# Two-layer trunk on one core: operands of six early pairs before the right sums, later turns, and two of four W sums on POOL

## The chip, the cores and the metric

The kernel runs on one core of one Trainium2 chip. The core has five engines with a queue of instructions each: PE (TensorE, the matmuls), DVE (VectorE), ACT (ScalarE), POOL (GpSimd) and SP (SyncE, which here only issues DMAs). An engine takes its queue strictly in order; an instruction that waits for a semaphore holds up all behind it. The metric is device microseconds of one execution, lower is better; the value compared is the median of the runs.

## The reference, cut to what matters

A decoder trunk: 1024 tokens of width 1024, two layers. Layer 0 mixes tokens with a sparse attention (NSA), layer 1 with sliding-window attention with sinks (SWA); each is followed by a squared-ReLU MLP of hidden width 4096. All is float32.

```python
def squared_relu_mlp(h, w_up, w_down):
    a = jax.nn.relu(h @ w_up)
    return (a * a) @ w_down

for i in range(DEPTH):                       # DEPTH = 2
    ...                                      # mod = adaLN of the condition, six parts
    h = modulate(rms_norm(x, norm_g[i, 0]), sh1, sc1)
    y = nsa_mixer(h, ...) if i % N_MIXERS == 0 else swa_sink_mixer(h, ...)
    x = x + (1 + g1)[:, None, :] * rms_norm(y, norm_g[i, 1])
    h = modulate(rms_norm(x, norm_g[i, 2]), sh2, sc2)
    y = squared_relu_mlp(h, mlp_w_up[i], mlp_w_down[i])
    x = x + (1 + g2)[:, None, :] * rms_norm(y, norm_g[i, 3])
```

## The kernel before, in words

**Precision.** A float32 product is three matmuls (`mm3`, L572 to L574): each operand is split into a rounded part `hi` (a copy on ACT) and the rest `lo` (a subtraction), and hi*hi, lo*hi and hi*lo are summed.

**Tokens and tiles.** The tokens are 8 tiles of 128. When the attention of a tile is done, its output is projected, normed and added to x, and a second norm gives `xr` (`norm_stages`, L450 to L472). Then the tile is turned: PE transposes `xr` by 8 matmuls with the identity (L1234), and ACT scales and shifts it out of PSUM into the raw operand `hr` (L1245). The function `done` decides when: in before the turn's steps follow the norm by `DL` = 4 steps of the program, and the further ones by 1 step each.

**MLP up.** `h @ w_up` is done with one level of Strassen-Winograd: both operands are cut in 2x2 blocks, and seven products p = 1 to 7 take the place of eight. The blocks on the right side (R) are of tokens and depth: b11 and b21 are of tiles 0 to 3 (depth halves 0 and 1), b12 and b22 of tiles 4 to 7. R of p=1 is b11, of p=2 b21; p = 6, 5, 7 need the sums (b22 - (b12 - b11)), t1 = (b12 - b11) and (b22 - b12), p=3 needs b22, and p=4 needs b21 minus that of p=6. Each sum comes in two halves j of 128x1024 (`minus`, L1257), each R operand as hh on ACT (L1250) and hl on DVE (L1251). The left side (W) comes in 16 pairs of hidden blocks. A pair needs four sums of W blocks (`prep`, L1313, L1314, L1320 for p=7, L1324 for p=3, 128x512 each), and for each product a `wt`: hi on ACT (L1330), lo by a subtraction (L1331; on POOL for the early products, on DVE for the others). One product is 12 matmuls of 128x512. L1358 adds a product's PSUM bank on DVE into the pair's two accumulators `u` (a and b), ACT does the squared ReLU (L1370, L1371), and POOL adds the results up as the right side of the next Strassen level (`combine`: sx at L1403, sy at L1414), which SP stores.

**Order.** Products p=1 and p=2 need only tiles 0 to 3, so those of `PAIRS0` = 5 pairs (10 products) run first, while the last tiles are still normed and turned. Then come 6, 5, 7, 3, 4 of each of these pairs, then all seven of each later pair. `before(i)` places the preparation of product i + `AHEAD` (3) ahead of product i; `lead` holds what stands ahead of the first. Program order is only the start: the framework schedules each engine's queue by a simulated timeline, and the queues that result are fixed.

**Buffers.** W of a pair is loaded as two tiles of 512 KB by SP (L547), c=0 (w11, w21) into one of 3 "raw" buffers and c=1 (w12, w22) into one of 41 general slots of 4 KB per partition (`SLOTS`). R operands, `wt`, `u`, `sx` and early raw sums all live in the same slots. A slot is used again when the last reader of its tile is done; for an `sx` that is the landing of its store. In before the second tile of the third pair's W (`w_11048` in layer 0) stands in the slot of the first pair's accumulator b.

## Time and profile before

| what | value |
|---|---|
| runs | 2559.64, 2564.80, 2564.22 us; median 2564.22 us |
| profiled execution | 2561.28 us, span 2559.3 us, mean granted clock 0.972 |
| busy share | PE 94%, DVE 76%, ACT 55%, POOL 50% |
| attention and projection of layer 0, up to the first product of its MLP | up to about 889 us |
| MLP up of layer 0 | 889 to 1216 us |
| SWA attention of layer 1, with its turns | 1620 to 1930 us |
| MLP up of layer 1 | from about 1910 us |

PE is busy for most of the span. What can be won lies in the stretches where PE idles or runs at a lower clock. The profile's list of waits says what ended each idle time of PE, the timeline gives each instruction with its start and duration, and the table of stretches gives the granted clock (1.00 is 2.4 GHz, 0.50 is 1.2 GHz) beside the busy times.

### The profile page before, as it was taken

What the parts mean: (1) busy time and instruction counts of PE and PEld (TensorE: products, weight loads), DVE (VectorE), ACT (ScalarE), POOL (GpSimd) and SP (SyncE); (2) the same over time, 40 slices, a digit from 0 to 9 for tenths busy, and PEclk for the clock granted to TensorE, in tenths of its full rate; (3) what the DMA queues carried; (4) which work ended last, traced back from release to release, by engine and by line L of the source; (5) the groups of instructions that cost most, each with busy time, mean ns of one, the idle gap of its engine ahead of it and who ended that gap; (6) DMA issues with size and microseconds to landing.
All of it is one profiled execution on the core that took longest, in us unless ns stands there. A gap on an engine that the chain in (4) does not pass through costs nothing.

```text
span 2559.3 us, 36576 instructions
## 1 busy us (share of the span) xinstructions
PE 2396.3 (94%) x11974; PEld 1996.3 (78%) x11974; DVE 1946.4 (76%) x3751; ACT 1397.0 (55%) x2959; POOL 1274.1 (50%) x1256
## 2 busy tenths in 40 slices
PE   6989899999998979999999999889787999999997
PEld 4789788888887867778778887767676788888886
DVE  7965479999895579888899777477647876787656
ACT  4632368898983544444444454378765454445433
POOL 4420566565662255334955613477545543494433
PEclk9999999999999989999999999989899999999999
DMA  7367623122227536555988564452223555587754
GB/s 277 116 220 243 215 79 96 39 90 66 72 67 165 148 127 215 197 185 181 359 312 309 203 215 148 124 157 68 65 67 120 201 170 179 179 308 251 228 185 171
DMA packets 237205, 436.08 MB, mean 170 GB/s; under 512 B 19204, under 2 KB 120792, under 8 KB 237016
## 3 DMA queue, kind: packets, MB, share of 16 engines
q1 hardware_dynamic: 208216, 404.39, 47.3%
q0 software_dynamic: 28800, 29.36, 4.7%
q8 instruction: 94, 1.54, 0.2%
q14 instruction: 95, 0.78, 0.1%
HBM read 319.38 MB, written 114.31 MB: 169 GB/s over the span
## 4 chain that ended last, share of the span: by engine, by line
PE 58%; DVE 16%; DMA 10%; issue 6%; POOL 4%; ACT 4%; SPq 1%; DVEq 0%; POOLq 0%; ACTq 0%
PE b L574 14%; PE b L573 14%; PE b L572 14%; PE b L880 5%; PE b L903 5%; PE o L925 4%; DMA adaw<-in_ada_w_dram 3%; DVE wt L1331 2%; DVE p L884 2%; DMA w<-in_mlp_w_up_dram 2%; DMA w<-in_nsa_w_in_dram 1%; DMA wr<-in_mlp_w_down_dram 1%; DVE u L1358 1%; DVE pT L910 1%; DVE ada L323 1%
## 5 line engine op out<-in xcount | busy, mean ns | idle before, releaser
L574 PE MATMUL b<-hh,wt 128*128 128x512 f32 x896 | 350.8, 395 | 25.1 <-POOL wt L1331 21.2
L572 PE MATMUL b<-hh,wt 128*128 128x512 f32 x896 | 354.4, 396 | 9.8 <-ACT wt L1330 9.8
L573 PE MATMUL b<-st,st 128*128 128x512 f32 x896 | 349.5, 390 | 5.4 <-DVE st L1477 5.4
L573 PE MATMUL b<-hl,wt 128*128 128x512 f32 x896 | 352.4, 393 | 0.0
L574 PE MATMUL b<-st,st 128*128 128x512 f32 x896 | 348.3, 389 | 0.0
L572 PE MATMUL b<-st,st 128*128 128x512 f32 x896 | 332.5, 390 | 1.6 <-DVE u L1358 1.6
L888 ACT ACTIVATE p<-p,nm 128x256 f32<-128x256 f32 (+7 forms) x384 | 251.2, 660 | 59.0 <-DVE nm L884 57.8
L1028 POOL TENSOR_SCALAR p<-p,rl,nsam 128x640 f32<-128x640 f32 (+7 forms) x256 | 200.4, 796 | 137.8 <-DVE rl L1026 96.8
L1477 DVE TENSOR_TENSOR st<-sr,st 128x1024 fp32r<-128x1024 f32 (+1 forms) x128 | 193.3, 1510 | 77.5 <-ACT st L1476 76.1
L1403 POOL TENSOR_TENSOR sx<-u,u 128x512 f32<-128x512 f32 x64 | 106.2, 1660 | 273.0 <-ACT u L1371 224.8
L910 DVE TENSOR_TENSOR pT<-b,pT 128x512 fp32r<-128x512 f32 (+1 forms) x334 | 215.4, 657 | 27.6 <-ACT pT L909 27.4
L574 PEld LDWEIGHTS b<-hh,wt 128*128 128x128 f32 x896 | 170.3, 190 | 66.1 <-POOL wt L1331 22.9
L1370 ACT ACTIVATE u<-u 128x512 f32<-128x512 f32 x128 | 80.6, 630 | 244.6 <-DVE u L1358 244.5
L909 ACT ACTIVATE pT<-b 128x512 fp32r<-128x512 f32 (+1 forms) x334 | 187.2, 580 | 43.1 <-PE b L903 36.9
L572 PEld LDWEIGHTS b<-hh,wt 128*128 128x128 f32 x896 | 170.3, 190 | 50.4 <-ACT wt L1330 15.9
L1476 ACT ACTIVATE st<-sr 128x1024 fp32r<-128x1024 f32 (+1 forms) x128 | 122.2, 955 | 158.8 <-PE b L573 104.8
L573 PEld LDWEIGHTS b<-st,st 128*128 128x128 f32 x896 | 168.2, 188 | 42.6 <-DVE st L1477 8.2
L903 PE MATMUL b<-ident,p 128*128 128x128 f32 x1296 | 195.9, 277 | 5.0 <-DVE nm L884 4.1
L1477 DVE TENSOR_TENSOR st<-wr,st 128x1024 fp32r<-128x1024 f32 (+1 forms) x128 | 181.8, 1420 | 20.8 <-ACT st L1476 18.1
L573 PEld LDWEIGHTS b<-hl,wt 128*128 128x128 f32 x896 | 170.0, 190 | 35.0
L572 PEld LDWEIGHTS b<-st,st 128*128 128x128 f32 x896 | 168.2, 188 | 37.3 <-DVE u L1358 2.3
L574 PEld LDWEIGHTS b<-st,st 128*128 128x128 f32 x896 | 168.2, 188 | 34.7
(276 smaller groups left out, 6183.6 us busy)
## 6 DMA issues: line engine op xcount, KB each, us to landing
adaw<-in_ada_w_dram SPq DMA_DIRECT2D x96, 512.0 KB, 4.7
sr<-s SPq DMA_DIRECT2D x96, 512.0 KB, 4.8
wr<-in_mlp_w_down_dram SPq DMA_DIRECT2D x96, 512.0 KB, 6.0
w<-in_mlp_w_up_dram SPq DMA_DIRECT2D x74, 512.0 KB, 4.2
s<-sx SPq DMA_DIRECT2D x64, 512.0 KB, 5.1
x<-x SPq DMA_DIRECT2D x48, 512.0 KB, 4.1
s<-u SPq DMA_DIRECT2D x64, 256.0 KB, 2.1
we<-in_mlp_w_down_dram SPq DMA_DIRECT2D x64, 256.0 KB, 4.0
```

Source lines behind the costliest of these rows:

```text
L572: mm(out, s[0], m[0], start=first, stop=False)
L573: mm(out, s[0], m[1], start=False, stop=False)
L574: mm(out, s[1], m[0], start=False, stop=last)
L880: self.nc.tensor.matmul(out, q[:, g], k[z], start=z == 0, stop=z == 1)
L888: self.nc.scalar.activation(p, p, AF.Exp, scale=-1.0, bias=nm, accum_out=l)
L903: nc.tensor.transpose(pt[:, g * P:(g + 1) * P], p[:, cols], self.ident)
L909: nc.scalar.activation(x[:, 0, 0:w], pt[:, 0:w], AF.Copy)
L910: nc.vector.tensor_tensor(x[:, 1, 0:w], pt[:, 0:w], x[:, 0, 0:w].bitcast(F32), op=ALU.subtract)
L1028: nc.gpsimd.tensor_scalar(ps[g], ps[g], rl[:, g:g + 1], gate[:, g, b:b + 1], op0=ALU.mult, op1=ALU.mult)
L1403: nc.gpsimd.tensor_tensor(z[n][:, k], x, y, op=op)
L1476: nc.scalar.activation(hi, r, AF.Copy)
L1477: nc.vector.tensor_tensor(lo, r, hi.bitcast(F32), op=ALU.subtract)
```

## The change

It has six parts. (1) `SLOTS` goes from 41 to 40, and three small tensors of the NSA attention move from a slot into constants. (2) `PAIRS0` goes from 5 to 6, so 12 products run first; the raw W of pairs 3 to 5 stands in slots, the W operands of the early products are prepared earlier (`when`), and their lo part is made on DVE. (3) The sums t1 and b22 - b12 are made tile by tile as tiles 4 to 7 are turned (`near`, pieces of 128x256, one on DVE and one on POOL for each j); after the last tile only b11 (DVE, twice 128x1024) and b21 (POOL, twice) are left. (4) The turn of a tile follows its norm by `TURN` = 10 steps in layer 0 and 20 in layer 1 (6 for the last tile). (5) Of the four W sums of each of the 16 pairs, those for p=7 and p=3 are made on POOL. (6) The side work (adaLN of later stages) is spread over the products from the 23rd on and not from the 11th.

```diff
--- before.py
+++ after.py
@@ -26,10 +26,11 @@
 HID = 4096
 EPS = 1e-6
 NEG = -1e30
-SLOTS = 41
+SLOTS = 40
 UT = HID // P
 LEAD_DOWN = 14
-PAIRS0 = 5
+PAIRS0 = 6
+TURN = (10, 20)
 SIDE2 = 40
 AHEAD = 3
 DL = 4
@@ -209,10 +210,9 @@
 
     def setup_late(self):
         nc, a = self.nc, self.a
-        both = self.slot("nsac")
-        self.pe = both[0:32, 0:256].rearrange("p (m z d) -> p m z d", m=2, z=2)
-        self.w2 = both[:, 256:768].rearrange("p (m c z d) -> p m c z d", m=2, c=2, z=2)
-        self.Kc = both[:, 768:1024].rearrange("p (h n) -> p h n", h=4)
+        self.pe = self.const([32, 2, 2, 64], "pe")
+        self.w2 = self.const([P, 2, 2, 2, 64], "w2")
+        self.Kc = self.const([P, 4, 64], "Kc")
         for z in range(2):
             nc.sync.dma_start(self.pe[:, :, z, :], a["nsa_cmp_pe"][0].rearrange("m l d -> l m d"))
             for m in range(2):
@@ -1256,19 +1256,28 @@
                 raw[out] = self.slot("hr", F32, [P, 2, 512])
             eng.tensor_tensor(raw[out], raw[x], raw[y], op=ALU.subtract)
 
+        b11, b21, b12, b22, t1 = (lambda j, n=n: (*n, j) for n in ((0, 0), (0, 1), (1, 0), (1, 1), (2, 0)))
+
+        def near(t, j):
+
+            if t1(j) not in raw:
+                raw[t1(j)] = self.slot("hr", F32, [P, 2, 512])
+            v = lambda n: raw[n][:, :, (t - 4) * P:(t - 3) * P]
+            nc.vector.tensor_tensor(v(t1(j)), v(b12(j)), v(b11(j)), op=ALU.subtract)
+            nc.gpsimd.tensor_tensor(v(b12(j)), v(b22(j)), v(b12(j)), op=ALU.subtract)
+
         def tile(t, xr):
             steps = [lambda c=c: (turn(t, xr, c), put(t, c)) for c in range(2)]
-            if t == 3:
-                steps += [lambda c=c, j=j: split((1, 2)[c], raw[0, c, j]) for c in range(2) for j in range(2)]
+            if t > 3:
+                steps.append(lambda: (near(t, 0), near(t, 1)))
             if t == 7:
                 V, G = nc.vector, nc.gpsimd
-                b11, b21, b12, b22, t1 = (lambda j, n=n: (*n, j) for n in ((0, 0), (0, 1), (1, 0), (1, 1), (2, 0)))
-                steps.append(lambda: [minus(e, *f(j)) for f in (lambda j: (t1(j), b12(j), b11(j)), lambda j: (b11(j), b22(j), t1(j)))
-                                      for j, e in ((0, V), (1, G))])
-                steps += [lambda j=j: (split(6, raw[b11(j)]), minus(G, b12(j), b22(j), b12(j))) for j in range(2)]
-                steps += [lambda j=j: (split(5, raw.pop(t1(j))), minus(G, b21(j), b21(j), b11(j)), raw.pop(b11(j))) for j in range(2)]
-                for p, b in ((7, b12), (3, b22), (4, b21)):
-                    steps += [lambda p=p, b=b, j=j: split(p, raw.pop(b(j))) for j in range(2)]
+                steps.append(lambda: [minus(V, b11(j), b22(j), t1(j)) for j in range(2)])
+                for p, b in ((6, b11), (5, t1), (7, b12), (3, b22)):
+                    if p == 5:
+                        steps.append(lambda: [minus(G, b21(j), b21(j), b11(j)) for j in range(2)])
+                    steps += [lambda p=p, b=b, j=j: split(p, raw[b(j)]) for j in range(2)]
+                steps += [lambda j=j: split(4, raw[b21(j)]) for j in range(2)]
             return steps
 
 
@@ -1283,7 +1292,7 @@
 
         def load(q, early):
             if early:
-                r = self.raw_weight(self.raw, w_up, list(range(KT)), 2 * q * P, P)
+                r = self.raw_weight(self.raw if q < 3 else self.slot, w_up, list(range(KT)), 2 * q * P, P)
                 r = r.rearrange("p (k c) -> p k c", k=KT)
                 wraw[q] = {11: r[:, 0:4], 12: r[:, 4:8]}
             else:
@@ -1306,7 +1315,7 @@
                 return sums[n]
 
             if p == 1:
-                r = w[11] if early else w[11]
+                r = w[11]
             elif p == 2:
                 r = w[12]
             elif p == 6:
@@ -1317,35 +1326,38 @@
                 r = sums.pop(1)
             elif p == 7:
                 r = new(3)
-                t(r, w.pop(11), w.pop(21), op=ALU.subtract)
+                nc.gpsimd.tensor_tensor(r, w.pop(11), w.pop(21), op=ALU.subtract)
                 sums.pop(3)
             elif p == 3:
                 r = new(4)
-                t(r, w.pop(12), sums.pop(2), op=ALU.subtract)
+                nc.gpsimd.tensor_tensor(r, w.pop(12), sums.pop(2), op=ALU.subtract)
                 sums.pop(4)
             else:
                 r = w.pop(22)
             s = self.slot("wt", F32R, [P, 2, 512])
             hi, lo = (four(s[:, y]) for y in range(2))
             nc.scalar.activation(hi, r, AF.Copy)
-            (nc.gpsimd if early else nc.vector).tensor_tensor(lo, r, hi.bitcast(F32), op=ALU.subtract)
+            nc.vector.tensor_tensor(lo, r, hi.bitcast(F32), op=ALU.subtract)
             left[i] = s
             if early and p == 2 or p == 4:
                 wraw.pop(q)
 
+
+        first = at[0]
+        when = lambda i: -1 if i < 3 else (i - 3) // 2 if i < first else max(i - first + 5, i - AHEAD) if i < first + 5 else i - AHEAD
+
         def before(i):
 
-            out = []
-            n = i + AHEAD
-            if 0 <= n < len(order):
-                out.append(lambda: prep(n))
-            out += [lambda q=q: load(q, True) for q in range(2, PAIRS0) if n == 4 * (q // 2) + q % 2 - 3]
+            out = [lambda n=n: prep(n) for n in range(len(order)) if when(n) == i]
+            if i in (0, 1, 2):
+                out += [lambda q=q: load(q, True) for q in (3 + i,) if q < PAIRS0]
             for q in range(n_q):
-                if n == at[q] - 2:
+                if i == (2 if q == 0 else when(at[q] - 2)):
                     out.append(lambda q=q: load(q, False))
             return out
 
-        lead = [lambda q=q: load(q, True) for q in range(2)] + [f for i in range(-AHEAD, 0) for f in before(i)]
+        lead = [lambda q=q: load(q, True) for q in range(3)] + [lambda j=j: split(1, raw[b11(j)]) for j in range(2)] + \
+            before(-1) + [lambda j=j: split(2, raw[b21(j)]) for j in range(2)]
         return tile, (R, order, before, left, lead)
 
     def mlp_up(self, up, side, sd, begin):
@@ -1423,7 +1435,7 @@
             own = spread(before(i), product(i))
             if p == 4:
                 own.append(lambda q=q: self.later(lambda: self.chain(combine(q)), 1))
-            (ramp if i < 2 * PAIRS0 else steps).extend(own)
+            (ramp if i < 2 * PAIRS0 + 10 else steps).extend(own)
         self.go(ramp)
         self.go(spread(side, steps[:-LEAD_DOWN]) + spread(begin, steps[-LEAD_DOWN:]))
 
@@ -1709,10 +1721,9 @@
 
             take, up = self.up_setup(a["mlp_w_up"][l], lambda l=l: self.cols[l, 1])
 
-            def done(t, x, take=take, xr=xr):
+            def done(t, x, take=take, xr=xr, l=l):
                 def turn():
-                    for k, f in enumerate(take(t, xr)):
-                        self.later(f, DL if k == 0 else 1)
+                    self.chain([lambda: None] * (2 + DL if t == NT - 1 else TURN[l]) + take(t, xr))
                 self.chain(self.norm_stages(x, xr, t) + [turn])
 
             if l == 0:
@@ -1731,7 +1742,6 @@
                     return {26: loads[0:1], 27: loads[1:2], 28: loads[2:3], 29: loads[3:5], 30: loads[5:6], 31: loads[6:]}.get(n, [])
 
                 self.nsa_attention(more, parts[-1][1][QN:])
-                self.pe = self.w2 = self.Kc = self.Vc = self.cmask = self.fmask = self.gate = None
                 outs = [self.out_steps(t, lambda t=t: load(t), src[t], gate, x1[t], done) for t in range(NT)]
                 self.mark("wout")
                 outs[0][0]()
```

On POOL at the entry of layer 0's MLP, before (`hr` are raw operands and their sums, `wt` the lo part of an early product, `sx` and `sy` the first pair's results):

```order
L1331 TENSOR_TENSOR wt2399_10684<-w2382_10582,wt2399_10684 128x512
L1257 TENSOR_TENSOR hr2405_10725<-hr2351_10424,hr2240_9919 128x1024
L1257 TENSOR_TENSOR hr2350_10421<-hr2353_10432,hr2350_10421 128x1024
L1257 TENSOR_TENSOR hr2240_9919<-hr2354_10435,hr2405_10725 128x1024
L1257 TENSOR_TENSOR hr2351_10424<-hr2354_10435,hr2351_10424 128x1024
L1257 TENSOR_TENSOR hr2242_9927<-hr2242_9927,hr2239_9916 128x1024
L1331 TENSOR_TENSOR wt2408_10734<-w2378_10547,wt2408_10734 128x512
L1257 TENSOR_TENSOR hr2243_9930<-hr2243_9930,hr2240_9919 128x1024
L1331 TENSOR_TENSOR wt2422_10780<-w2382_10582,wt2422_10780 128x512
```

The same place on POOL after (`ws` are the sums of W blocks of the first two pairs):

```order
L1267 TENSOR_TENSOR hr2344_10413<-hr2347_10430,hr2344_10413 128x2x128
L1267 TENSOR_TENSOR hr2345_10416<-hr2348_10433,hr2345_10416 128x2x128
L1257 TENSOR_TENSOR hr2259_10002<-hr2259_10002,hr2256_9985 128x1024
L1257 TENSOR_TENSOR hr2260_10005<-hr2260_10005,hr2257_9988 128x1024
L1329 TENSOR_TENSOR ws2450_10945<-w2413_10764 128x512
L1333 TENSOR_TENSOR ws2453_10966<-w2414_10766,ws2444_10906 128x512
L1329 TENSOR_TENSOR ws2467_11050<-w2457_10979 128x512
L1333 TENSOR_TENSOR ws2471_11074<-w2458_10981,ws2462_11009 128x512
L1426 TENSOR_TENSOR sy2478_11098<-u2391_10659,u2455_10971 128x512
L1415 TENSOR_TENSOR sx2470_11071<-u2391_10659,u2455_10971 128x512
```

No lo part of a `wt` stands behind the full-size sums any more, two of which are left; four W sums stand ahead of the first pair's results.

On PE in the SWA attention, at the turn of the third tile, before (`xr` is the normed tile, `b` a PSUM bank, L880, L903 and L925 are attention matmuls):

```order
L574 MATMUL b3980_18653<-wh3703_17478,ol3958_18577 128x512
L925 MATMUL o3978_18649<-pT3955_18569,V23534_16476 128x512
L1234 MATMUL b3981_18666<-ident_67,xr3975_18633 128x128 x4
L1234 MATMUL b3982_18675<-ident_67,xr3975_18633 128x128 x4
L880 MATMUL b3983_18684<-K23530_16472,qs3962_18586 128x256 x4
L880 MATMUL b3984_18685<-K23530_16472,qs3962_18586 128x256 x4
```

The same place on PE after, with the rows where that tile's turn now stands:

```order
L574 MATMUL b3980_18669<-wh3703_17494,ol3958_18593 128x512
L880 MATMUL b3997_18758<-K23530_16488,qs3962_18602 128x256 x4
L925 MATMUL o3993_18742<-pT3977_18662,V23534_16492 128x512
...
L574 MATMUL b4003_18782<-wh3752_17674,ol3958_18593 128x512
L1234 MATMUL b4022_18881<-ident_67,xr3975_18649 128x128 x4
L1234 MATMUL b4024_18899<-ident_67,xr3975_18649 128x128 x4
```

The turn of `xr3975` went 36 rows down the list (a row being one matmul or a group of like ones), behind the next tile's projection products.

On SP in layer 0's MLP up, the issue of the second W tile of the third pair and what stands around it, before:

```order
L1415 DMA s2387_0_10621<-sy2476_11051 128x512
L547 DMA w2516_11289<-in_mlp_w_up_dram 128x4x256
L1409 DMA s2387_0_10621<-sx2468_11024 128x1024
L547 DMA w2475_11048<-in_mlp_w_up_dram 128x4x256
L1412 DMA s2387_0_10621<-sx2473_11043 128x1024
```

After:

```order
L1427 DMA s2387_0_10636<-sy2478_11098 128x512
L1421 DMA s2387_0_10636<-sx2470_11071 128x1024
L547 DMA w2477_11095<-in_mlp_w_up_dram 128x4x256
L1424 DMA s2387_0_10636<-sx2475_11090 128x1024
```

The place is nearly the same, but the buffer is another. `w2477_11095` stands in the slot that `sx2470_11071` leaves, so its load waits for the landing of the store one row above it, where before it waited for POOL's last read of an accumulator. Layer 1 has the same (`w_20251` in the slot of `sx_20227`; before, `w_20186` took the slot of an old `wt`). The second tile of the fourth and of the fifth pair stands in the slot of the accumulator b of two pairs earlier, in both layers.

## Rows read from the trace of the kernel before

**Rows 1.** The page: its first line, the span and the count of instructions.
```profile
span 2559.3 us, 36576 instructions
```
**Rows 2.** Timeline of POOL, 893 to 928 us: start, duration, engine, line, names, idle before.
```profile
899.97 14.99 POOL L1257 TENSOR_TENSOR hr<-hr,hr 128x1024 f32<-128x1024 f32 x5 [2.19 <-ACT hr L1245]
914.93 2.25 POOL L1331 TENSOR_TENSOR wt<-w,wt 128x512 fp32r<-128x512 f32 x1
```
**Rows 3.** Timeline of PE, 895 to 966 us, the turn and the instructions after idle times.
```profile
897.75 1.03 PE L1234 MATMUL b<-ident,xr 128*128 128x128 f32 x8
...
917.24 0.80 PE L574 MATMUL b<-hh,wt 128*128 128x512 f32 x1 [9.82 <-POOL wt L1331]
...
926.78 0.50 PE L572 MATMUL b<-hh,wt 128*128 128x512 f32 x1 [0.94 <-ACT wt L1330]
...
933.70 0.50 PE L572 MATMUL b<-hh,wt 128*128 128x512 f32 x1 [1.63 <-ACT wt L1330]
...
965.59 0.50 PE L572 MATMUL b<-hh,wt 128*128 128x512 f32 x1 [2.42 <-ACT wt L1330]
```
**Rows 4.** Stretches: bounds, length, busy (PE PEld DVE ACT POOL), PEclk, DMA share, GB/s.
```profile
907.00:922.00 15.00, 5.18 (x14) 3.67 (x12) 11.67 (x6) 9.68 (x12) 15.00 (x6) 0.66 0.16 52
...
935.00:939.00 4.00, 4.00 (x11) 3.13 (x12) 2.29 (x4) 2.53 (x6) 0.00 (x0) 0.57 1.01 344
...
963.00:970.00 7.00, 4.58 (x13) 3.28 (x13) 6.51 (x10) 3.73 (x7) 3.28 (x2) 0.76 0.38 132
```
**Rows 5.** Timeline of DVE, 894 to 898 us, the last tile's xr.
```profile
895.86 0.75 DVE L472 TENSOR_SCALAR xr<-x,r 128x1024 f32<-128x1024 f32 x1 [1.02 <-POOL r L451]
```
**Rows 6.** Waits of PE, 1925 to 1965 us: total, times, longest.
```profile
PE b L574 <- POOL wt L1331: 10.9, 2, 9.8
PE b L572 <- ACT wt L1330: 2.6, 2, 1.6
```
**Rows 7.** Stretch of layer 1's MLP entry, columns as in rows 4.
```profile
1932.00:1947.00 15.00, 5.19 (x16) 3.55 (x14) 11.67 (x6) 9.36 (x11) 15.00 (x6) 0.66 0.16 52
```
**Rows 8.** Waits of PE, 1735 to 1890 us, columns as in rows 6.
```profile
PE b L1234 <- DVE xr L472: 15.7, 4, 5.1
```
**Rows 9.** Stretches of the SWA attention, columns as in rows 4.
```profile
1740.00:1890.00 150.00, 125.68 (x655) 105.84 (x655) 100.54 (x283) 112.71 (x313) 95.03 (x141) 0.91 0.25 64
...
1802.00:1809.00 7.00, 4.80 (x23) 4.80 (x24) 3.25 (x12) 4.35 (x14) 1.27 (x2) 0.52 0.02 8
...
1833.00:1840.00 7.00, 5.06 (x25) 5.07 (x26) 3.30 (x12) 4.33 (x11) 1.01 (x2) 0.51 0.00 0
```
**Rows 10.** Timeline of POOL, 949 to 959 us, the first pair's results in layer 0.
```profile
953.11 1.30 POOL L1414 TENSOR_TENSOR sy<-u,u 128x512 f32<-128x512 f32 x1 [1.24 <-ACT u L1371]
954.36 2.29 POOL L1403 TENSOR_TENSOR sx<-u 128x512 f32<-128x512 f32 x1
...
957.85 1.30 POOL L1403 TENSOR_TENSOR sx<-u 128x512 f32<-128x512 f32 x1
```
**Rows 11.** Timeline of SP, 942 to 975 us, the issue of w_11048.
```profile
957.92 0.38 SPq L547 DMA_DIRECT2D w<-in_mlp_w_up_dram  x1
```
**Rows 12.** Timeline of DVE, 953 to 969 us, the third pair's first W sum.
```profile
963.46 0.69 DVE L1313 TENSOR_TENSOR ws<-w,w 128x512 f32<-128x512 f32 x1 [1.73 <-DMA w<-in_mlp_w_up_dram]
```
**Rows 13.** The page's DMA issues: count, KB each, median us from issue to landing.
```profile
w<-in_mlp_w_up_dram SPq DMA_DIRECT2D x74, 512.0 KB, 4.2
s<-sx SPq DMA_DIRECT2D x64, 512.0 KB, 5.1
```
**Rows 14.** Groups of instructions by shape, 850 to 1215 us: busy, mean ns, idle before.
```profile
L1403 POOL TENSOR_TENSOR sx<-u,u 128x512 f32<-128x512 f32 x28 | 46.9, 1674 | 133.8 <-ACT u L1371 110.0 <-PE b L574 8.4 <-DMA s<-sx 5.7
...
L1324 DVE TENSOR_TENSOR ws<-w,ws 128x512 f32<-128x512 f32 x16 | 20.6, 1291 | 0.0
L1320 DVE TENSOR_TENSOR ws<-w 128x512 f32<-128x512 f32 x16 | 15.8, 990 | 0.0
```
**Rows 15.** A stretch of layer 0's MLP up, columns as in rows 4.
```profile
1050.00:1100.00 50.00, 50.00 (x221) 41.14 (x220) 42.37 (x48) 23.26 (x41) 22.85 (x15) 1.00 0.61 195
```

## The prediction

> **What bounds the kernel now.** I read the list of PE's waits first, then PE's timeline at the places it names, then the queues of the engines named there, and last the table of stretches for the granted clock. PE is busy for most of the span [rows 1], so what counts is where it idles and who ended the idle time. Three places bear on this change.
>
> At the entry of layer 0's MLP, PE runs out of products. It waits 9.82 us for the lo part of an early W operand, then 0.94 and 1.63 us for hi parts [rows 3], 12.39 us in all. The 9.82 us are one queue: POOL works through five full-size right sums for 14.99 us, and only then comes to the small `wt` (2.25 us) for which PE waits [rows 2]. After that wait the granted clock is low: 0.66 over the stretch with PE busy for 5.18 us of it, all but a fraction at 1.2 GHz, and 0.57 over 4 us after the 1.63 us wait [rows 4]. Work at half clock takes twice the time, so about 2.3 + 1.7 = 4.0 us are lost beside the idle time: 16.4 us.
>
> Layer 1's entry is a copy: 10.9 us for POOL and 2.6 us for ACT [rows 6], and about 2.2 us of clock [rows 7]: 15.7 us.
>
> In the SWA attention, PE waits four times for the `xr` of a turn, 15.7 us [rows 8], and two of these waits are followed by 7 us at 0.52 and 0.51, with 4.80 and 5.06 us busy [rows 9], so (4.80 + 5.06) / 2 = 4.9 us more: 20.6 us.
>
> **The change, part by part.** The sum is made against the profiled execution, 2561.28 us (2.0 us beside its span); the median of the runs, 2564.22, is 2.9 us above it, and I add that at the end.
>
> *Entry of layer 0.* Right sums go tile by tile, the lo parts leave POOL, and 12 products stand ready and not 10. After the last turn DVE still has two sums and ten hl parts of 128x1024; a sum of half that size takes 0.69 us [rows 12], so twelve need 16.6 us, and some 20 with POOL's two sums in between (an estimate). The products that cover them last 12 x 2.72 = 32.6 us (12 matmuls each, 50 us / 221 apart [rows 15]), of which about 26 stand behind that turn. I expect the three waits to go: 16.4 us. One thing comes back. The last tile's turn now stands behind two products and not three, so PE reaches it at 897.75 - 2.72 = 895.0, while `xr` was done at 895.86 + 0.75 = 896.6 [rows 3, 5]; and its norm now stands behind more copies on ACT and pieces of sums on DVE, which I put at 2.7 us. PE then waits 4.3 us (between 1.6 and 6) and loses about 1 us of clock. Net -11.1 us, between -6 and -16.
>
> *Entry of layer 1.* The same, but the last turn stands later here; three small waits come back, some 1.9 us by the queue's order. Net -13.8 us, between -7 and -16.
>
> *Later turns in the SWA attention.* A turn 36 rows further down has its `xr` long before PE arrives, so the 15.7 us of waits go as such. How much remains saved is the most doubtful term. In the 150 us from 1740 to 1890 PE is busy for 125.68 us, ACT for 112.71, DVE for 100.54, POOL for 95.03 [rows 9]. Squeezed by 20.6 us, ACT would be at 87%, in chains of softmax steps with order fixed on each queue; and the pauses of PE at the turns are the time in which these engines now catch up. I take a little over half, -12 us, between -3 and -20.
>
> *A new wait for W in the early pairs.* The second W tile of the third pair is now loaded into the slot of the first pair's first `sx`. Call E the end of the first pair's last product; in the trace of before PE ran without a gap from there to the third pair's first product, five products long, so E = 963.0 - 13.6 = 949.4 (965.59 less the wait of 2.42 is 963.2) [rows 3]. Now the third pair's W must be ready at E + 13.6. POOL takes up the first pair's results when the squared ReLU is done, at 953.11 in the trace, E + 3.7 [rows 10]. In the new order that is sy, then two halves of sx, 1.30 us each, or up to 2.29 [rows 10]: done at E + 7.6 to 8.7. The store lands 5.1 us after its issue and the load 4.2 us after its own [rows 13] (the load of before, issued at 957.92, landed at about 963.4, 5.5 us) [rows 11, 12]. From landing to PE's start it took 965.59 - 963.46 = 2.1 us [rows 3, 12]. That makes E + 19.0 to 21.4, so PE waits 5.4 to 7.8 us; since the engines may come to the results a little sooner with less queued, I take 6, and 1.4 for the clock (after 2.42 us PE ran at 0.76 [rows 4]). The fifth pair's second tile stands in the slot of the third pair's accumulator b, which is the case that cost 2.42 us and about 1.1 of clock in before: again 2.5 and 1.4. The fourth pair's has the same kind of slot, but gains the 6 us by which PE is late. So 11.3 us per layer. Layer 0 already paid 3.5 of it; layer 1 paid none, its tile having stood in the slot of an old `wt`. Net +7.8 and +11.3 = +19.1 us, between +3 (the store's landing met in time) and +32 (each of these waits 50% longer, and the fourth pair late as well).
>
> *Two sums of four on POOL.* 32 instructions of a layer leave DVE, where those at L1324 and L1320 took 1.29 and 0.99 us on average [rows 14], longer than the 0.69 us of the like sum at L1313 with POOL idle [rows 12]: DVE is held up while POOL runs. On POOL each costs 1.30 us alone, 1.67 in company [rows 10, 14]. In a steady stretch DVE is busy for 42.37 of 50 us and POOL for 22.85 [rows 15]; POOL has room, and the sums are asked for three products (8.2 us) ahead. In the five-product pairs the two engines together come to about 14.5 us of sums and splits in 13.6 us of PE, if they never overlap: 4 pairs x 0.9 x 2 layers is 7 us at worst. I take +4, between 0 and +12 (below zero is possible only where DVE is what PE waits for, which no wait beyond 0.5 us in these stretches shows).
>
> *At nothing:* the constants for a slot, the side work's later start and the earlier loads. SP, POOL and DVE have idle time where these lie; one slot less is priced above in the waits for slots.
>
> Sum: -11.1 - 13.8 - 12 + 19.1 + 4 = -13.8 us; 2561.3 - 13.8 = 2547.5, and 2.9 more for the median: **2550 us**.
>
> **The rivals.** (A) *The W waits don't arise.* If the squared ReLU and POOL come to the first pair 4 us sooner than in before, since DVE has less queued, the load comes about as late as before, and both layers pay the old 3.5 us: +3.5 and not +19.1, so 2534 us. For: DVE loses 1.29 + 0.99 us per pair. Against: store and load alone take 9.3 us of the 13.6.
>
> (B) *The SWA turns bring nothing.* PE waits as long, for softmax steps and not for `xr`: 2550 + 12 = 2562. For: ACT at 87%. Against: ACT, DVE and POOL each idle for 37 us or more of the 150 [rows 9].
>
> (C) *Starved early pairs, slower than before.* The waits for slots are not two per layer but follow at each of pairs three to six, as each late load delays the results that free the next slot. At 6 + 1.4 us for four pairs in two layers that is 59 us, less the old 3.5: +56 and not +19.1, so 2587 us. It decides from where the early pairs cost more than about 20 us per layer. For: three second tiles per layer now wait for POOL's results of two pairs earlier. Against: each wait of PE gives the loads behind it the same time.
>
> (D) *DVE and POOL exclude one another.* The rows show it in part: L1324's 1.29 against 0.69 us alone [rows 12, 14]. If that port were full, every sum moved would cost 1.30 - 0.69 = 0.61 us more of it, 32 x 2 x 0.61 = 39 us in place of my 4: 2585 us. Against: DVE's additions from PSUM (L1358) don't take part, and with them left out the steady stretch is not full. The Trainium skill (Perfetto Trace Analysis, "Optimizing Scalar/DVE Operations") states this rule: the two engines share a read port of SBUF, so moving operations between them might not help. The trace agrees that they hold each other up; that the sums find no room, no row shows.
>
> **How the numbers follow.** Forecast as summed 0.48, A 0.24, B 0.12, C 0.10, D 0.06. The forecast's own range by its terms is 2537 to 2562. Faster than 2559 by over 0.2% (about what a measurement here can tell): A, most of the forecast (0.42) and a little of B: 0.68. Within 0.2% (2559 to 2569): the rest of the forecast and most of B: 0.15. Slower: C, D and a bit: 0.17. The range leaves out C and D and the better part of A's lower tail: 2528 to 2570.
>
> **What would show it.** In the changed profile: no wait of PE for a `wt` from POOL at either entry; a turn of the last tile with a wait of some 4 us near 895 in layer 0; no wait of L1234 for `xr` in SWA, and other waits there summing to about 8 us more than before; at the third pair of both layers a wait of about 6 us for the hi part, ended by a W load that was issued just after the landing of an `sx`, and one of 2 to 3 us at the fifth. I am wrong if the third pair starts without a wait (A), if the SWA stage keeps its length (B), or if DVE or POOL is busy throughout the five-product pairs and PE waits in every one (C, D).

## The result, and the profile after

The changed kernel takes 2548.18 us (median of 4 runs, 2545.86 to 2549.94) against 2563.11 for the kernel before; the ratio is 0.9943, with a 95% interval of 0.9931 to 0.9955. The forecast was 2550. The profiled execution took 2548.21 us, with this span and these busy times (page, first lines):

```profile
span 2546.4 us, 36695 instructions
PE 2399.9 (94%) x11974; PEld 1991.6 (78%) x11974; DVE 1924.9 (76%) x3723; ACT 1403.2 (55%) x2959; POOL 1325.5 (52%) x1308
```

The total came out near the forecast, its parts did not. The next table is worked out from PE's timelines: where a stage's first or last matmul stands in the two profiled executions. The 1344 matmuls of a layer's MLP up are counted in order, 12 to a product.

| stage | before, us | after, us | difference | forecast |
|---|---|---|---|---|
| start, to the first matmul of layer 0's output projection | 793.4 | 796.2 | +2.8 | 0 |
| from there to the end of product 12 of layer 0's MLP | 147.9 | 145.2 | -2.7 | -11.1 |
| products 13 to 112, layer 0 | 289.1 | 297.8 | +8.7 | +7.8, and half of +4 |
| MLP down, layer 0 | 324.5 | 326.6 | +2.1 | 0 |
| SWA stage, to the end of product 12 of layer 1's MLP | 410.1 | 373.3 | -36.8 | -25.8 |
| products 13 to 112, layer 1 | 275.9 | 289.5 | +13.6 | +11.3, and half of +4 |
| the rest | 318.5 | 317.8 | -0.7 | 0 |

Up to the end of layer 0 the change loses 11 us, and after it wins 24. (The 2.1 us in layer 0's MLP down were not followed further. Layer 0's MLP up ends at 1230 us before; the 1216 in the table of the kernel before is too early.) Each row is one profiled execution against another, so a difference of a microsecond or two says little.

The bound behind product 12 needs a word. Before, PE's waits at the entry of an MLP (behind POOL's queue of right sums, and for the first right product) fall on products 7 to 11; after, those at the first right products fall on products 13 to 17, and so into the rows of products 13 to 112. Products 13 to 17 take 13.6 us in both layers before, which is five products without a wait, and 17.1 us in layer 0 and 20.7 us in layer 1 after. With the bound drawn behind product 17 the same executions read as follows, and these are the numbers to hold against the forecast:

| stage | difference, us | forecast |
|---|---|---|
| layer 0, from the projection to the end of product 17 | +0.8 | -11.1 |
| products 18 to 112, layer 0 | +5.2 | +7.8, and half of +4 |
| SWA stage, to the end of product 17 of layer 1 | -29.7 | -25.8 |
| products 18 to 112, layer 1 | +6.5 | +11.3, and half of +4 |

Where the 9.82 us wait of [rows 3] stood, PE's timeline after (885 to 1010 us) shows this; the bracket at a row's end is the idle time and what ended it:

```profile
894.33 1.09 PE L1234 MATMUL b<-ident,xr 128*128 128x128 f32 x8 [0.62 <-DVE xr L472]
898.42 0.54 PE L572 MATMUL b<-hh,wt 128*128 128x512 f32 x1 [2.08 <-ACT wt L1339]
910.62 1.97 PE L1234 MATMUL b<-ident,xr 128*128 128x128 f32 x8 [4.79 <-DVE xr L472]
943.85 0.50 PE L574 MATMUL b<-hh,wt 128*128 128x512 f32 x1 [1.99 <-DVE wt L1340]
...
975.29 0.50 PE L572 MATMUL b<-hh,wt 128*128 128x512 f32 x1 [2.49 <-ACT wt L1339]
...
990.77 0.50 PE L572 MATMUL b<-hh,wt 128*128 128x512 f32 x1 [1.28 <-ACT wt L1339]
995.47 0.50 PE L574 MATMUL b<-hh,wt 128*128 128x512 f32 x1 [2.92 <-DVE wt L1340]
```

No wait for POOL is left. There is the wait of the last turn (4.79 us; 4.3 were forecast), a crowd of small ones ahead of it, and after the 12 products one of 1 to 3 us in nearly every pair. The third pair's wait (975.29) is 2.49 us and not 6; the fifth's (1009.77, forecast 2.5) is 1.07 us, and in layer 1 2.60 us. In SWA the answer to [rows 8, 9] is a list of waits (1725 to 1900 us) with no turn in it, and a fuller PE:

```profile
PE b L572 <- DVE oh L1179: 2.5, 1, 2.5
PE b L574 <- DVE ol L1180: 2.2, 1, 2.2
PE b L880 <- DVE nm L884: 1.6, 2, 1.3
PE b L572 <- DVE nm L884: 0.9, 2, 0.7
```
```profile
1740.00:1890.00 150.00, 141.20 (x767) 117.67 (x766) 107.53 (x315) 122.38 (x344) 100.43 (x160) 0.97 0.28 74
```

PE is busy for 141.2 of 150 us (125.7 before) with ACT at 122.4, 82%.

### The profile page after: what moved, and what is told of

It is laid out like the page before. It is cut to its first block, busy times and chain, and to the rows that moved or that the text cites. A ratio compares the mean times of both kernels' runs of the same rounds, so it can differ in the third digit from the quotient of the medians.

```text
span 2546.4 us, 36695 instructions
## 1 busy us (share of the span) xinstructions
PE 2399.9 (94%) x11974; PEld 1991.6 (78%) x11974; DVE 1924.9 (76%) x3723; ACT 1403.2 (55%) x2959; POOL 1325.5 (52%) x1308
## 4 chain that ended last, share of the span: by engine, by line
PE 40%; DVE 6%; POOL 3%; issue 2%; DMA 2%; ACT 2%; SPq 0%; POOLq 0%; DVEq 0%; ACTq 0%
PE b L574 13%; PE b L572 13%; PE b L573 12%; POOL sx L1415 1%; DVE ada L323 1%; PE b L880 1%; DMA w<-in_mlp_w_up_dram 1%; DVE hl L1251 1%; PE o L925 1%; DVE p L884 1%; PE b L903 1%; DVE wt L1340 1%; DMA adaw<-in_ada_w_dram 0%; POOL qv L637 0%; POOL wr L1473 0%
## 5 line engine op out<-in xcount | busy, mean ns | idle before, releaser
L572 PE MATMUL b<-hh,wt 128*128 128x512 f32 x896 | 355.0, 396 | 17.0 <-ACT wt L1339 16.9
L574 PE MATMUL b<-hh,wt 128*128 128x512 f32 x896 | 350.9, 395 | 11.9 <-DVE wt L1340 11.6
L573 PE MATMUL b<-st,st 128*128 128x512 f32 x896 | 350.3, 391 | 4.9 <-DVE st L1489 4.9
L573 PE MATMUL b<-hl,wt 128*128 128x512 f32 x896 | 352.1, 393 | 0.0
L572 PE MATMUL b<-st,st 128*128 128x512 f32 x896 | 330.7, 390 | 1.6 <-DVE u L1370 1.6
L910 DVE TENSOR_TENSOR pT<-b,pT 128x512 fp32r<-128x512 f32 (+1 forms) x334 | 215.0, 657 | 19.5 <-ACT pT L909 19.1
L1488 ACT ACTIVATE st<-wr 128x1024 fp32r<-128x1024 f32 (+1 forms) x128 | 122.6, 958 | 193.2 <-POOL wr L1474 87.4
L1489 DVE TENSOR_TENSOR st<-wr,st 128x1024 fp32r<-128x1024 f32 (+1 forms) x128 | 188.3, 1471 | 53.6 <-ACT st L1488 30.1
L1489 DVE TENSOR_TENSOR st<-sr,st 128x1024 fp32r<-128x1024 f32 (+1 forms) x128 | 200.4, 1566 | 33.0 <-ACT st L1488 30.8
L572 PEld LDWEIGHTS b<-hh,wt 128*128 128x128 f32 x896 | 170.1, 190 | 59.3 <-ACT wt L1339 25.4
L573 PEld LDWEIGHTS b<-st,st 128*128 128x128 f32 x896 | 168.5, 188 | 42.4 <-DVE st L1489 7.8
L903 PE MATMUL b<-ident,p 128*128 128x128 f32 x1296 | 193.5, 273 | 5.7 <-DVE nm L884 4.1
L1340 DVE TENSOR_TENSOR wt<-ws,wt 128x512 fp32r<-128x512 f32 x128 | 139.5, 1101 | 77.4 <-ACT wt L1339 76.8
L572 PEld LDWEIGHTS b<-st,st 128*128 128x128 f32 x896 | 168.6, 188 | 37.2 <-DVE u L1370 2.4
L573 PEld LDWEIGHTS b<-hl,wt 128*128 128x128 f32 x896 | 170.1, 190 | 34.6
L925 PE MATMUL o<-pT,kv 128*128 128x512 f32 x484 | 193.1, 437 | 1.8 <-DVE pT L910 1.4
```

What stands on the lines that cost most here:

```text
L572: mm(out, s[0], m[0], start=first, stop=False)
L573: mm(out, s[0], m[1], start=False, stop=False)
L574: mm(out, s[1], m[0], start=False, stop=last)
L903: nc.tensor.transpose(pt[:, g * P:(g + 1) * P], p[:, cols], self.ident)
L910: nc.vector.tensor_tensor(x[:, 1, 0:w], pt[:, 0:w], x[:, 0, 0:w].bitcast(F32), op=ALU.subtract)
L925: nc.tensor.matmul(out, s, m[:, z], start=n == 0 and z == 0, stop=n == len(tiles) - 1 and z == 1)
```

## The experiments

Times are medians; the kernel before, run beside them, took 2562.8 to 2564.5. In kernels that have the NSA tensors in a slot, lines of the profile stand one higher than in the changed kernel (L573 for L572).

**The turns of layer 1 alone**, in the kernel before, for tiles 0 to 5 (the change delays tile 6 as well):

```diff
                 def turn():
+                    if l == 1 and t < NT - 2:
+                        self.chain([lambda: None] * 20 + take(t, xr))
+                        return
```

> The kernel before with one part of the change: the turns of tiles 0 to 5 in layer 1 follow the norm by 20 steps and not 4. Theory: nearly all of the 15.7 us of waits for xr and of the 4.9 us of low clock behind them are saved, and no other wait takes their place: 2543 to 2547 us. Rival: the softmax engines use the pauses, half or more comes back as other waits: 2552 to 2560 us.

2547.61 us, ratio to the kernel before 0.9930 (0.9911 to 0.9951), so 16.2 us less: alone worth as much as the whole change (14.9). From the end of layer 0's MLP to product 12 of layer 1 it takes 394.9 us, 15.3 less than before. Its stretch and its longest waits in SWA (1725 to 1890 us):

```profile
1740.00:1890.00 150.00, 137.13 (x726) 112.37 (x725) 105.10 (x291) 118.56 (x327) 95.43 (x147) 0.97 0.26 70
```
```profile
PE b L572 <- DVE oh L1179: 2.8, 1, 2.8
PE b L880 <- DVE nm L884: 2.6, 3, 1.1
PE b L572 <- DVE nm L884: 2.0, 3, 0.7
```

Some waits for softmax steps came back, about 4 us over the stage, but not half of what went. Rival B is out.

**The turns of layer 0 back**, in the changed kernel:

```diff
-TURN = (10, 20)
+TURN = (4, 20)
```

> The changed kernel with the turns of layer 0 following the norm by 4 steps again, as before, and those of layer 1 still by 20; all else as changed. In the changed profile layer 0's first product of its MLP starts at 898.4 us and not at 889.5. Theory: 6 us of that come from the later turns (waits of 0.6 to 2.1 us and a low clock from 880 to 898, because the last tiles' norms, turns and copies now crowd together), so the first product starts near 892 and the kernel takes about 2542 us, against 2548 for the change. Rival: the late start lies in the 780 us ahead of this stage and in the early operands' order, so the time stays within 2 us of 2548.

2539.21 us, 9.0 less. The first product starts at 895.6 us, 2.8 earlier and not 6 as the theory had it. Product 12 of layer 0 ends 140.4 us after the first matmul of the projection, against 145.2 in the changed kernel and 147.9 before; products 13 to 17 then take 18.9 us against 17.1, so at product 17 the gain is 3.1 us. PE's timeline, 865 to 911 us, now has the turns' waits and nothing else:

```profile
870.25 1.06 PE L1234 MATMUL b<-ident,xr 128*128 128x128 f32 x8 [2.37 <-DVE xr L472]
...
889.23 1.09 PE L1234 MATMUL b<-ident,xr 128*128 128x128 f32 x8 [0.66 <-DVE xr L472]
...
904.77 1.09 PE L1234 MATMUL b<-ident,xr 128*128 128x128 f32 x8 [3.53 <-DVE xr L472]
```

So the later turns, which bring 16 us in SWA, cost layer 0's entry 3 to 5. The likely reason: its tiles follow each other about every 12 us without an attention between them, and a delay only pushes the last turns onto the entry; no run takes that apart. The rest of the 9 us lies in a start 1.2 us earlier, in products 18 to 112 of layer 0 (2.3 us) and in layer 1 (1.8 us).

**One slot more, the NSA tensors in a slot again** (parts of (1) undone), and **the tensors in a slot but 40 slots**:

```diff
-SLOTS = 40
+SLOTS = 41
...
-        self.pe = self.const([32, 2, 2, 64], "pe")
-        self.w2 = self.const([P, 2, 2, 2, 64], "w2")
-        self.Kc = self.const([P, 4, 64], "Kc")
+        both = self.slot("nsac")
...
```

> The changed kernel with 41 slots and the three small NSA tensors in one of them again, so that one slot more is free from the MLP on; all else as changed. Theory slots: the second W tile of the third pair finds another slot or is loaded earlier, and products 13 to 42 take 4 to 10 us less in each layer: 2530 to 2540 us. Rival, the sums on POOL and the order on DVE: within 3 us of 2548.

> The changed kernel with 40 slots as changed, but the three small NSA tensors in one of them as before, and not in constants. In the seven profiles with the slot the first product of layer 0's output projection starts at 789.5 to 793.4 us, in the three with constants at 795.0 to 796.2. Theory: the constants let the small loads go ahead of the adaLN weights at the start, which costs some 4 us there, and the number of slots alone costs the early pairs: the start comes back to about 791.5, products 13 to 42 still take some 98 us per layer, and the time is 2543 to 2546 us. Rival: the start differs by chance, and what 41 slots brought was all in the early pairs: 2548 us. Second rival: a slot fewer shows at the start too: the start stays at 795.

2540.36 us with 41 slots, and 2542.92 with 40. So 5.3 us of the gain are the constants, and 2.6 the slot; the runs with 40 slots spread from 2540.15 to 2546.62, so this split is sure to some 2 us only. The constants' share lies at the very start. SP's timeline of the changed kernel, 20 to 60 us, has the small loads ahead of x and of the rope tables:

```profile
27.58 1.80 SPq L219 DMA_DIRECT2D w<-in_nsa_phi_w_dram  x2
...
39.65 2.70 SPq L1656 DMA_DIRECT2D x<-in_x_dram  x4
43.38 4.01 SPq L299 DMA_DIRECT2D rope<-turn  x4
```

In the kernel before, the same stretch has them behind:

```profile
35.81 2.69 SPq L1644 DMA_DIRECT2D x<-in_x_dram  x4
38.61 6.74 SPq L299 DMA_DIRECT2D rope<-turn  x4
...
45.88 1.27 SPq L219 DMA_DIRECT2D nsac<-in_nsa_phi_w_dram  x2
```

With 40 slots and the tensors back in one, the projection starts early again (PE, 789 to 797 us):

```profile
789.57 0.77 PE L573 MATMUL b<-wh,oh 128*128 128x512 f32 x1 [6.54 <-DVE oh L1180]
```

Over all profiles it starts at 789.5 to 793.4 us with the slot and at 795.0 to 796.2 with constants. Most of that is lost by 70 us: PE's 200th matmul starts at 65.2 to 67.4 us in the ten profiles with the slot and at 68.8 to 69.6 in the three with constants, while the 100th, at 43.6 to 46.1, shows no difference. The slot itself shows in layer 0's early pairs. Waits of PE over products 13 to 42, with 40 slots (936 to 1038 us), then with 41 (937 to 1031 us):

```profile
PE b L573 <- ACT wt L1340: 6.5, 5, 2.5
PE b L575 <- DVE wt L1341: 5.8, 4, 2.9
```
```profile
PE b L575 <- DVE wt L1341: 5.1, 4, 1.6
PE b L573 <- ACT wt L1340: 2.3, 1, 2.3
```

With 41, the third pair's second W tile stands in an accumulator's slot and the fourth's and fifth's in those of used `wt`, so the third pair no longer waits, and DVE's waits for W loads in this stretch fall from 7.6 to 3.8 us: products 13 to 42 of layer 0 are 7.5 us shorter. Of these, 4.6 us are lost again in products 43 to 112, which take 201.9 us and not 197.3; why, was not followed. In layer 1 the slot gives 1.2 us only.

**All W sums on DVE** in the changed kernel, and **the two sums on POOL** in the kernel before:

```diff
-                nc.gpsimd.tensor_tensor(r, w.pop(11), w.pop(21), op=ALU.subtract)
+                t(r, w.pop(11), w.pop(21), op=ALU.subtract)
...
-                nc.gpsimd.tensor_tensor(r, w.pop(12), sums.pop(2), op=ALU.subtract)
+                t(r, w.pop(12), sums.pop(2), op=ALU.subtract)
```

> The changed kernel with all four sums of W blocks of a pair on DVE, as before; all else as changed. In the changed profile products 13 to 42 (the six five-product pairs) take 98.3 us in layer 0 and 98.5 us in layer 1, where 30 products without a wait are 81.5 us. Theory slots: the waits come from second W tiles that stand in slots which POOL's results free late, so they stay within 3 us per layer and the kernel takes 2545 to 2550 us. Rival, the sums: POOL's queue and DVE's lo parts hold each other up, and the waits shrink by 8 us or more per layer, to 2532 us or less.

> The kernel before with one part of the change: the W sums for p=7 and p=3 on POOL. Theory of the prediction: POOL's sums cost a few us in the early pairs and nothing later, 2565 to 2575 us. Rival, from the run with all sums on DVE (10.8 us slower than the change): DVE is the tighter engine, and the kernel before gains as well, 2553 to 2560 us. Third: the kernel before has no wait in the later pairs that the sums could shorten, so it stays within 2 us, and what the sums bring in the changed kernel is tied to its other parts.

The changed kernel without POOL's sums takes 2558.97 us, 10.8 more, which neither theory had. The kernel before with them takes 2564.95, ratio 1.0014 (1.0003 to 1.0025): some 2 to 4 us more. Both effects of the sums are there at once. In the changed kernel with the sums on DVE, products 13 to 42 get shorter, by 2.0 us in layer 0 and by 5.9 in layer 1; but in the later pairs PE then waits for DVE, and products 43 to 112 take 11.5 us more in layer 0 and 7.2 more in layer 1. Its waits over layer 0's later products (1037 to 1240 us), with the sums on DVE and then as changed:

```profile
PE b L574 <- DVE wt L1340: 5.5, 4, 2.5
PE b L349 <- DVE adas L345: 5.1, 3, 2.8
```
```profile
PE b L574 <- DVE wt L1340: 2.8, 1, 2.8
PE b L349 <- DVE adas L345: 1.6, 2, 1.0
```

**The two undone parts together**, `TURN = (4, 20)` and 41 slots:

> The changed kernel with the turns of layer 0 at 4 steps and with 41 slots (the NSA tensors in one of them), together. Alone the two gave 2539.2 and 2540.4 us, against 2548.2. If the two gains lie in different places (the turns at the entry of layer 0; the slot at the start of the program and in the early pairs) they add: 2530 to 2533 us. Rival: both only give the early pairs of layer 0 more time, so one is worth little beside the other: 2537 us or more.

2528.82 us (2528.67 to 2529.81), ratio to the kernel before 0.9864 (0.9846 to 0.9883): the two gains add, with some 2 us to spare, and this version is 19.4 us faster than the change and some 34 faster than before.

**On top of that version, the sums on DVE** (the same edit as above):

> The changed kernel with layer 0's turns at 4 steps and 41 slots (2528.8 us), and with all four W sums on DVE. Theory: the sums on POOL are worth what they were in the changed kernel, since DVE is then the tighter queue in the later pairs too: 2536 to 2542 us. Rival: with enough slots DVE's waits go, as in the kernel before, where the sums on POOL gave nothing: 2527 to 2531 us.

2532.32 us, 3.5 more and between the two theories: with a slot more and the earlier turns, most of DVE's trouble goes, not all.

**On top of it, the right sums at full size after the last turn:**

```diff
-            if t > 3:
-                steps.append(lambda: (near(t, 0), near(t, 1)))
...
+                steps.append(lambda: [minus(e, t1(j), b12(j), b11(j)) for j, e in ((0, V), (1, G))])
+                steps.append(lambda: [minus(G, b12(j), b22(j), b12(j)) for j in range(2)])
                 steps.append(lambda: [minus(V, b11(j), b22(j), t1(j)) for j in range(2)])
```

> The changed kernel with layer 0's turns at 4 steps and 41 slots, and with the right sums t1 and b22 - b12 made at full size after the last turn (one of t1 on DVE, one on POOL, both b22 - b12 on POOL) and not tile by tile. Theory: the sums tile by tile are what takes POOL's 15 us off the entry, so each layer's first right product waits 4 to 9 us longer: 8 to 18 us slower than with them. Rival: the lo parts on DVE and the 12 products ahead do it, and the sums have room behind them: within 3 us.

2543.00 us, 14.2 more: of all parts tried on their own, this one and the turns of layer 1 are worth most. In the profiles the loss lies at the entries (9.8 us in layer 0 and 3.3 in layer 1, by product 17). In layer 0, PE waits 5.4 us at product 13 and not 1.7, and the granted clock over products 13 to 17 is 0.77 and not 1.00. Its POOL timeline (895 to 945 us) shows the queue at the entry:

```profile
906.90 5.25 POOL L1258 TENSOR_TENSOR hr<-hr,hr 128x1024 f32<-128x1024 f32 x2 [0.96 <-ACT hr L1246]
913.32 6.14 POOL L1258 TENSOR_TENSOR hr<-hr,hr 128x1024 f32<-128x1024 f32 x2 [1.16 <-DVE hr L1258]
919.41 2.30 POOL L1330 TENSOR_TENSOR ws<-w 128x512 f32<-128x512 f32 x1
926.42 6.20 POOL L1334 TENSOR_TENSOR ws<-w,ws 128x512 f32<-128x512 f32 x1 [4.70 <-DVE ws L1324]
```

**On top of it, five early pairs** (`PAIRS0 = 5`):

> The changed kernel with layer 0's turns at 4 steps and 41 slots, and with 5 early pairs and not 6. Theory: two products less (5.4 us) cover the right operands, which needed 2 to 4 us more than 12 products give (waits of 0.9 and 2.1 us at the first right product of layer 0, 2.0 and 0.6 in layer 1), so each entry waits about 5 us longer, and one five-product pair less gives 2 us back: 5 to 8 us slower. Rival: the slots of the sixth pair are what the early pairs lack, and their waits of about 10 us per layer halve: 3 to 8 us faster.

2529.17 us, the same. Both mechanisms are there, and they cancel. By the profiles the sixth pair brings 3.7 us in layer 0 (from the projection to the end of the MLP up) and costs 5.2 in layer 1. In layer 1 with five pairs, PE waits longer at the first right product and then, over all the early pairs, not once (1920 to 2000 us):

```profile
PE b L573 <- ACT wt L1340: 6.4, 1, 6.4
PE b L575 <- DVE wt L1341: 1.5, 1, 1.5
```

With six pairs it waits there for 3.2 us, and then for some 5 us in the pairs behind. In the kernel with five pairs, the second W tiles of the third to fifth pair all stand in slots of used `wt`.

**On top of it, the side work from the 13th product on** (`i < 2 * PAIRS0` for the ramp):

> The changed kernel with layer 0's turns at 4 steps and 41 slots (2528.8 us), and with the side work spread from the 13th product on and not from the 23rd. Theory: the adaLN steps on DVE stand in the way of the lo parts in the early pairs, so putting them there costs them 3 to 6 us, and the later pairs get 2 to 4 back: 2528 to 2533 us. Rival: spread thinner they disturb less everywhere: 2522 to 2527 us.

2537.91 us, above both theories, but the four runs spread from 2531.13 to 2538.91, and the profiled one is the lowest. In it products 13 to 112 take 3.7 us more in layer 0 and 4.0 less in layer 1. What made the other three slower stands in no profile, so this part of the change stays open. Of part (2), the lo parts of the early products on DVE and their earlier preparation were not run on their own either.

## Why the prediction was right, and where its steps were not

*The time and its sign* came out, at 2548 for 2550, and that is luck in good part: errors of about 16 us either way cancelled. Layer 0's entry brought nothing in place of 11.1 us, and the start and MLP down, put at nothing, cost 4.9. Against that the products behind the entries (18 to 112) cost 11.7 us and not 23.1, and SWA with layer 1's entry brought 4 us more.

*Entry of layer 0* (-11.1 forecast, +0.8 measured by product 17). That POOL's queue would go was right, and the wait of the last turn was of the forecast size (4.79 for 4.3). The step that failed is "I expect the three waits to go": they went, but others came, and PE's waits from the projection to the end of product 17 sum to 11.9 us against 12.9 before. Two causes show. One is the reach of the change: I weighed the later turns for SWA and, in layer 0, only their effect on the last tile's norm. The run with `TURN` at 4 shows 3 to 5 us that they cost there. The other is DVE, whose ten hl parts took the place of POOL's queue, with 1.99 us at the first right product. (With the turns at 4 steps and 41 slots the entry takes 7.4 us less than before; so the parts of the change are worth most of the forecast there when these two don't stand in the way.) DVE at layer 0's entry (930 to 948 us):

```profile
938.61 3.98 DVE L1251 TENSOR_TENSOR hl<-hr,hh 128x1024 fp32r<-128x1024 f32 x2
...
943.12 1.88 DVE L1340 TENSOR_TENSOR wt<-ws,wt 128x512 fp32r<-128x512 f32 x3
```

In layer 1, DVE's timeline (1929 to 1946 us) runs without a pause up to the lo part that PE awaits (0.62 us; PE waits 1.98 and 0.79 us more for hi parts, on an ACT whose own waits from 1930 to 1940 us are all for DVE):

```profile
1929.07 1.21 DVE L1251 TENSOR_TENSOR hl<-hr,hh 128x1024 fp32r<-128x1024 f32 x1
...
1931.41 4.57 DVE L1251 TENSOR_TENSOR hl<-hr,hh 128x1024 fp32r<-128x1024 f32 x2
...
1942.24 1.21 DVE L1251 TENSOR_TENSOR hl<-hr,hh 128x1024 fp32r<-128x1024 f32 x1
1943.37 0.68 DVE L1340 TENSOR_TENSOR wt<-ws,wt 128x512 fp32r<-128x512 f32 x1
```

Two of the parts took 4.57 us in place of 2.4, just while POOL made the early W sums (its timeline, 1929 to 1936 us):

```profile
1930.96 1.68 POOL L1333 TENSOR_TENSOR ws<-w,ws 128x512 f32<-128x512 f32 x1 [4.11 <-DVE ws L1323]
1932.60 2.29 POOL L1329 TENSOR_TENSOR ws<-w 128x512 f32<-128x512 f32 x1
```

Two more took 5.70 us (from 1922.24), beside POOL's last right sum and its first W sum. That fits the run with all sums on DVE, in which only two of layer 1's hl parts are stretched so (4.56 us, beside a right sum) and the first pair of layer 1 loses 4.3 us less (products 13 to 17).

*SWA and layer 1's entry* (-25.8 forecast, -29.7 measured by product 17). The mechanism was right. The turns alone gave 15.3 us in this stage for the 12 forecast; if the two add, 14.4 are left for the entry, for which I had 13.8. What was a little too small is the share of the 20.6 us that I kept. I took just over half because ACT would be near its limit, at 87%; in the run of the turns alone ACT is busy for 118.56 of 150 us, 79%, and the longest waits of PE are for DVE.

*The new wait for W* (+19.1). The third pair's wait was sized 6 us; it is 2.49 in layer 0, and in layer 1 it isn't there. Call E again the end of the first pair's last product (958.5 and 1959.9 us). Two steps were mis-sized. The first is the store's 5.1 us, a median over the whole program: on SP (963 to 985 us) the load that waits for the store's landing goes out 2.7 us after the store, and DVE waits for it:

```profile
965.41 0.32 SPq L1421 DMA_DIRECT2D s<-sx  x1
968.09 0.38 SPq L547 DMA_DIRECT2D w<-in_mlp_w_up_dram  x1
```
```profile
972.62 0.69 DVE L1322 TENSOR_TENSOR ws<-w,w 128x512 f32<-128x512 f32 x1 [2.48 <-DMA w<-in_mlp_w_up_dram]
```

The second is the time of the results. I had `sx` done at E + 7.6 to 8.7; in layer 0 its store goes out at E + 6.9, in layer 1 at E + 3.4. With the same 2.7 us behind it, DVE reads the W of layer 1 at E + 10.2, in time for the third pair at E + 13.6 (SP, 1955 to 2000 us, and DVE, 1965 to 1985 us):

```profile
1963.34 0.32 SPq L1421 DMA_DIRECT2D s<-sx  x1
1966.02 0.38 SPq L547 DMA_DIRECT2D w<-in_mlp_w_up_dram  x1
```
```profile
1970.13 0.69 DVE L1322 TENSOR_TENSOR ws<-w,w 128x512 f32<-128x512 f32 x1
```

The term and the half of the next came to +5.2 and +6.5 for +9.8 and +13.3, out of many waits of 0.4 to 2.9 us. What makes them is settled in part. In layer 0 the slot is most of what the early pairs lose: products 13 to 42 take 12.0 us more than in the kernel before with 40 slots, and 4.5 with 41; over products 13 to 112 the slot is worth 3.0. In layer 1 the waits behind the entry come with the sixth pair: with five, in the version with the earlier turns and 41 slots, there is none. The sums on POOL make products 13 to 42 of layer 1 5.9 us longer, but 4.3 of these are the entry's.

*Two sums on POOL* (+4). In the kernel before they cost what I had said, about 2 to 4 us. In the changed kernel they save 10.8. My reason against a gain was that no wait in these stretches of the trace of before is for DVE by more than 0.5 us. That leaves out one of 2.73 us for a lo part in a later pair (at 1149.22); still, by the run, the kernel before has nothing to gain there; the same change takes a slot away and moves the side work, and in that kernel DVE is waited for. With the slot back and the earlier turns, 3.5 us remain. How much the side work has to do with it stays open.

*At nothing* (the constants). They cost 4 to 5 us at the start. Loads that no longer wait for a slot went ahead in SP's queue, and x is issued 3.8 us later (39.65 for 35.81); that this order is the cause fits the times, but no run changes the order alone. The prediction saw moved instructions from the projection on alone; SP's queue changes at 27 us already.

*The rivals.* B fell with the run of the turns alone. C is there in small: nearly every early pair waits, and products 13 to 42 take 17 us more than 30 products without a wait in each layer (3.5 and 7.1 of it at the entry), below the 20 from which C was to decide. D is half true: DVE and POOL do hold each other up, yet there was room. A's reason, results ready earlier, is what spared layer 1 the wait together with the store's landing; in layer 0 the landing did more.

## What to carry to other kernels

Price a delay stage by stage: the same later turn won 16 us where other work stood between the tiles and lost 3 to 5 where it did not. Follow every buffer that changes its pool back to the queue that loads it, since a load that waits for nothing may pass one that matters. And put a part's price to the kernel that the other parts leave behind: the moved sums cost 2 us in the old kernel and saved 11 in the new one. And when a change moves a wait from one side of a measuring point to the other, move the point before comparing: here that turned -2.7 into +0.8 and -36.8 into -29.7.

## What the runs showed of the hardware

POOL's sum of 128x512 took 1.30 us while DVE was idle (957.85 in [rows 10]), 6.23 us at layer 0's entry of the changed kernel (at 933.03), and 6.20 us in the version without the sums tile by tile, both while DVE worked through its hl parts at 1.2 us each. DVE in that version, 924 to 934 us:

```profile
926.26 2.35 DVE L1252 TENSOR_TENSOR hl<-hr,hh 128x1024 fp32r<-128x1024 f32 x2
928.53 0.68 DVE L1341 TENSOR_TENSOR wt<-w,wt 128x512 fp32r<-128x512 f32 x1
929.14 2.35 DVE L1252 TENSOR_TENSOR hl<-hr,hh 128x1024 fp32r<-128x1024 f32 x2
```

Elsewhere it was the other way round: a DVE part of 1.21 us took 2.3 beside POOL's sums. So, as far as the overlap in time shows, either of the two can be held up, POOL here for more than four times its length. That agrees with the rule of the Trainium skill (Perfetto Trace Analysis, "Optimizing Scalar/DVE Operations") that they share a read port of SBUF. Its caution that moving operations between them might not help came true in the kernel before (2.1 us more) and not in the changed kernel, where PE waited for DVE's queue (10.8 us less).
